# Strassen's seven products over half of K in three gates in place of one; the gated sum h in DRAM between the gates, the score tiles in a slot

## The chip, the core and the metric
The kernel runs on one core of a Trainium2 chip: TensorE (matmul), VectorE, ScalarE, GpSimd, and SyncE, whose queue issues most DMAs. The metric is the device time of one execution in microseconds, the median of several runs.

## What is computed
One layer of a hybrid decoder for 512 prompt rows and 8 x 4 = 32 sample rows, together 544 rows, with D = 2048 and branch width 512, in float32. Cut to what matters here:

```python
z = x @ w_in                       # 12 projections of 512 columns, 4 forget columns, 4 gates of 2048 columns
h = 0
for i, (o, g) in enumerate(branches):         # gMLP, convolution, FoX attention, memory attention
    gate = sigmoid(gate_pre[:, i*2048:(i+1)*2048])       # a (544 x 2048) @ (2048 x 2048) product each
    h = h + gate * ((o * silu(g)) @ w_branch[i])         # (544 x 512) @ (512 x 2048)
y = layer_norm(ALPHA * x + h @ w_out)
```
FoX attention of the sample rows reads 1024 past keys and values for each of 8 sequences from pages in DRAM.

## The kernel before
All matmuls take a weight tile of 128 x 128 as stationary operand and x transposed as moving operand, in two halves of 272 columns. Each float32 operand is split into a high and a low part, and a product is three matmuls (high-high, high-low, low-high).

**Pieces.** The work is a list of `Piece`s. A plain piece (`std_load`, `std_conv`, `std_mm`) is 256 rows of K by 256 output columns: 2 K tiles x 2 column tiles x 3 products x 2 halves = 24 matmuls, all at line 269. Its weights are loaded into `raw` (5 buffers) up to four pieces ahead of their split; ScalarE (L238) and VectorE (L239) split them into `whl` (4 buffers), three pieces ahead of their matmuls. A projection is 16 pieces. A gate (`add_gates`) is 8 blocks of 256 columns; a block is 8 pieces of the gate product (K = 2048) and 2 pieces of the branch product (K = 512). The accumulators are four PSUM banks, two for each column tile: the gate product leaves them through a sigmoid on ScalarE (L1034) into a tile `gs`, the branch product through a multiplication on VectorE (L1045 or L1047), and from the second gate on GpSimd adds the result to h (L1048). h lies in four slots of SBUF until the end.

**Strassen.** In six blocks of the last gate (`add_strassen`) the first half of K is done as a 2 x 2 block product in seven products in place of eight: pieces P1 to P4 in the order of `kinds`, 12 matmuls each (L387), then 4 plain pieces for the other half of K and 2 for the branch. Weight differences are made on VectorE (L358) from four `sw` tiles, the operands from x by `t_sx` (L335, 28 steps) in the first two blocks of that gate, into four slots.

**The order of the list**: Q_C, 4 forget columns, K_C, V_C, Q_M (16 pieces each), 32 pieces for the memory's keys and values, V_A, U_A, G_A (16 each), gate 0 (80), G_M (16), gate 3 (80), A_B, B_B, G_C (16 each), gate 2 (80), G_B (16), 4 pieces of the pointwise convolution, gate 1, the output projection. I name the gates by their number in the code: 0, 3, 2 and last 1.

**What runs between.** The order is written out by hand (`tc.manual_schedule`): all engines take their instructions in the order of the program. Ahead of a piece's matmuls two chains of side tasks (generators in `Side`) get steps: in a plain piece up to 2 of chain 0 and 1 of chain 1; a step that yields 1 ends its chain's turn for the piece. A third list, `side.vec`, is `v_scores`: 24 empty steps and then 1280 scores of the sample rows against their pages (one VectorE instruction each, L713), given out by `side.vector(rate)`: 4 per piece before gate 0, 5 after it, none in Strassen pieces, and one of two pieces in the memory's 32. It begins in the third piece of K_C. When the last score is issued, `t_decode("qc")` is added to chain 0: 5 steps for the bias (`t_bias`), 2 transposes, softmax, and from step 13 on 16 groups of V products (L865), each of two steps of one per piece. For every group GpSimd gathers four pages of V by indirect DMA (L884) into a slot, two groups ahead; the slots (18 of 8.7 KB per partition, for all large tiles) are given out in the order in which they come free. The first evacuation of G_C (`ev_gate`, L1004), at the end of its eighth piece, calls `side.finish` for the two attention tasks: what they have left is issued there at once. `t_b`, the convolution task (chain 1, from the end of B_B), makes 124 convolution steps (L1216, L1219), two to a step of the task, in G_C and gate 2, with no steps in pieces that follow the end of a product; behind them its tail (two means with jn, L1231 to L1236, square root, sigmoid). `t_a` is the gMLP's task in V_A to G_A.

## Time and profile before
| | us |
|---|---|
| median of 3 runs | 1955.72 |
| lowest, highest | 1955.38, 1957.82 |
| the profiled execution, its own time | 1958.77 |
| its span, first to last instruction | 1957.1 |
| TensorE busy | 1926.9 |
| VectorE busy | 1278.6 |

The profile is of one execution. Its page gives the busy time of each engine, the chain of work that ended last, and the costliest groups of instructions; the trace behind it answers for single stretches, lines and tiles. "Idle before" an instruction names what ended the wait. The engine names of the rows are PE (TensorE), PEld (its weight loads), DVE (VectorE), ACT (ScalarE), POOL (GpSimd) and SP (SyncE).

### The profile page before, as it was taken

The numbers are of one execution on the slowest core, as the hardware profiler recorded it, in microseconds if no ns is written. First come the engines' busy times: TensorE is split into PE (matmuls) and PEld (weight loads), VectorE is DVE, ScalarE is ACT, GpSimd is POOL, SyncE is SP. The second block draws the span as 40 slices with busy tenths as digits, with TensorE's granted clock in tenths as the row PEclk, the third lists the DMA queues.
The fourth block names the chain that finished last, engine by engine and source line by source line (L and its number), as shares of the span: only waits on it lengthen the run. The fifth ranks groups of instructions, "written<-read, shape, count | busy, mean of one in ns | idle before, by whom it ended". The sixth has DMA issues, their size and how long they took to land.

```text
span 1957.1 us, 38249 instructions
## 1 busy us (share of the span) xinstructions
PE 1926.9 (98%) x14615; PEld 1854.2 (95%) x14615; DVE 1278.6 (65%) x4201; ACT 642.2 (33%) x1208; POOL 233.3 (12%) x265
## 2 busy tenths in 40 slices
PE   8999999999999999999999999999999999999997
PEld 7999989999999899999999889999999999999985
DVE  3265787777776777877763238667645655466687
ACT  3222353344223222222222222222243333344442
POOL 0000000010000000121215430101110011010000
PEclk9999999999999999999999999999999999999999
DMA  5444465324555544444436663333323332346664
GB/s 162 107 119 119 137 199 148 104 77 128 166 168 171 183 136 116 138 131 123 138 105 193 191 194 86 88 87 88 91 76 87 103 96 67 108 130 216 201 216 159
DMA packets 217745, 261.84 MB, mean 134 GB/s; under 512 B 18251, under 2 KB 177499, under 8 KB 216761
## 3 DMA queue, kind: packets, MB, share of 16 engines
q1 hardware_dynamic: 206441, 224.55, 39.5%
q0 software_dynamic: 10544, 33.80, 5.6%
q8 instruction: 114, 1.87, 0.4%
q10 hardware_dynamic: 576, 1.05, 0.1%
q14 instruction: 70, 0.57, 0.1%
HBM read 250.85 MB, written 8.49 MB: 133 GB/s over the span
## 4 chain that ended last, share of the span: by engine, by line
PE 79%; DVE 4%; DMA 3%; issue 1%; ACT 1%; SPq 0%; POOL 0%; DVEq 0%; ACTq 0%; POOLq 0%
PE acc L269 65%; PE acc L1393 4%; PE acc L387 3%; PE acc L926 2%; DVE whl L239 1%; PE ps L865 1%; DMA raw<-in_w_out_dram 1%; DMA raw<-in_w_branch_dram 1%; DMA qb<-qqm 0%; DVE junk L713 0%; DMA vr<-in_cache_mem_v_dram 0%; PE ps L958 0%; ACT whl L238 0%; PE ps L979 0%; PE ps L616 0%
## 5 line engine op out<-in xcount | busy, mean ns | idle before, releaser
L269 PE MATMUL acc<-xh,whl 128*128 128x272 f32 x6784 | 1172.7, 291 | 3.2 <-DVE sg L1010 2.5
L269 PEld LDWEIGHTS acc<-xh,whl 128*128 128x128 f32 x6784 | 969.8, 190 | 22.5 <-ACT whl L238 7.5
L238 ACT ACTIVATE whl<-raw 128x512 fp32r<-128x512 f32 x640 | 403.0, 632 | 1045.8 <-PE acc L269 864.8
L269 PE MATMUL acc<-xl,whl 128*128 128x272 f32 x3392 | 702.1, 289 | 0.0
L239 DVE TENSOR_TENSOR whl<-raw,whl 128x512 fp32r<-128x512 f32 x640 | 445.3, 699 | 359.9 <-ACT whl L238 352.8
L269 PEld LDWEIGHTS acc<-xl,whl 128*128 128x128 f32 x3392 | 535.6, 189 | 0.0
L713 DVE CUSTOM_DVE_ANT_0 junk<-kr,qb 128x128 f32<-128x128 f32 x1280 | 379.6, 297 | 48.5 <-DMA qb<-qqm 7.6
L269 PE MATMUL acc<-bh,whl 128*128 128x272 f32 x1024 | 177.5, 289 | 2.0 <-ACT gs L1034 1.3
L1048 POOL TENSOR_TENSOR h<-h,gs 128x272 f32<-128x272 f32 x96 | 79.3, 855 | 602.0 <-DVE gs L1047 601.9
L269 PEld LDWEIGHTS acc<-bh,whl 128*128 128x128 f32 x1024 | 146.7, 189 | 3.8 <-ACT gs L1024 1.8
L884 POOL DMA_INDIRECT kr<-in_cache_k_dram,idx x64 | 65.7, 1027 | 683.6 <-DVE L L713 497.9
L269 PE MATMUL acc<-hh,whl 128*128 128x288 f32 x512 | 107.2, 299 | 0.2 <-DVE whl L239 0.2
L269 PE MATMUL acc<-bl,whl 128*128 128x272 f32 x512 | 105.7, 288 | 0.0
L1219 DVE SCALAR_TENSOR_TENSOR yb<-hb,wdwc,yb 128x512 f32<-128x512 f32 x120 | 93.4, 779 | 2.1
L269 PEld LDWEIGHTS acc<-hh,whl 128*128 128x128 f32 x512 | 83.5, 188 | 0.8 <-DVE whl L239 0.4
L713 DVE DVE_READ_ACCUMULATOR2_ANT L<- 128x1 f32 x1024 | 83.9, 82 | 0.0
L269 PEld LDWEIGHTS acc<-bl,whl 128*128 128x128 f32 x512 | 80.6, 189 | 0.0
L269 PE MATMUL acc<-hl,whl 128*128 128x288 f32 x256 | 75.6, 295 | 0.0
L884 POOL DMA_INDIRECT vr<-in_cache_v_dram,idx x64 | 65.4, 1023 | 57.2 <-PE ps L865 40.5
L1393 PE MATMUL acc<-whl,hh 128*128 128x512 f32 x216 | 68.1, 396 | 0.8 <-ACT whl L238 0.5
L239 DVE TENSOR_TENSOR whl<-sw,whl 128x512 fp32r<-128x512 f32 x42 | 33.2, 791 | 40.4 <-ACT whl L238 26.3
L1393 PEld LDWEIGHTS acc<-whl,hh 128*128 128x128 f32 x216 | 40.4, 189 | 10.2 <-ACT whl L238 1.0
(350 smaller groups left out, 1425.1 us busy)
## 6 DMA issues: line engine op xcount, KB each, us to landing
raw<-in_w_in_dram SPq DMA_DIRECT2D x422, 256.0 KB, 2.8
raw<-in_w_out_dram SPq DMA_DIRECT2D x128, 256.0 KB, 3.6
raw<-in_w_branch_dram SPq DMA_DIRECT2D x64, 256.0 KB, 2.7
qb<-qqc SPq DMA_DIRECT2D x32, 256.0 KB, 4.1
qb<-qqm SPq DMA_DIRECT2D x32, 256.0 KB, 4.0
sw<-in_w_in_dram SPq DMA_DIRECT2D x24, 256.0 KB, 4.6
raw<-in_w_mem_k_dram SPq DMA_DIRECT2D x16, 256.0 KB, 2.7
raw<-in_w_mem_v_dram SPq DMA_DIRECT2D x16, 256.0 KB, 3.4
```

The lines of the kernel that those rows point to most:

```text
L238: S.activation(out=hi, in_=src, func=AF.Copy)
L239: side.later(lambda: V.tensor_tensor(out=lo, in0=src, in1=hi.bitcast(F32), op=ALU.subtract))
L269: T.matmul(out=p.st[c][i][:, 0:hi - lo], lhsT=p.w[:, wp, k, c * 128:(c + 1) * 128], rhs=mv[mp][:, p.k0 + k, lo:hi], start=(p.first or (c, ...
L387: T.matmul(out=acc, lhsT=p.w[:, wp, i, :], rhs=mv, start=p.kind in ("P1", "P2", "P5") and i == 0 and wp == 0 and mp == 0, stop=i == n - 1 ...
L713: V.tensor_tensor_reduce(out=junk, in0=kr[:, n % 2, h * 128:(h + 1) * 128], in1=qb[:, t, h * 128:(h + 1) * 128], op0=ALU.mult, op1=ALU.add ...
L865: T.matmul(out=ob[32 * j:32 * j + 32, :], lhsT=PT[:, pg, 4 * g + j, :], rhs=vr[:, j, :], start=pg == 0, stop=pg == npg - 1 and not fox)
L884: G.indirect_dma_start(out=dst, out_offset=None, in_=src, in_offset=bass.IndirectOffsetOnAxis(ap=idx[:, j:j + 1], axis=0))
L926: T.matmul(out=mem["a", p.wi, j], lhsT=m[:, mp, (2 * (p.kt % 2) + j) * 128:(2 * (p.kt % 2) + j + 1) * 128], rhs=p.w[:, wp], start=p.kt == ...
L1048: G.tensor_tensor(out=hd, in0=hd, in1=s, op=ALU.add)
L1219: V.scalar_tensor_tensor(out=yv, in0=hv, scalar=wdw[:, j, c:c + 1], in1=yv, op0=ALU.mult, op1=ALU.add)
L1393: T.matmul(out=oacc[p.nb, j], lhsT=hhl[p.kt // 4][mp][:, p.kt % 4, o:o + 128], rhs=p.w[:, wp], start=p.kt == 0 and mp == 0 and wp == 0, st ...
```

## The change
- Strassen over the first half of K in all 8 blocks of gate 3, in blocks 1 to 6 of gate 2 and in blocks 1 to 7 of gate 1 (`STR`): 21 blocks in place of 6. The operands are made once, by `t_sx` in gate 0 from its 56th piece on, and stay in four slots.
- h is no longer kept in SBUF: each block's 128 x 1088 part is stored to DRAM (`hscr`) some pieces after the block's end and loaded at the start of the same block of the next gate, into a ring of two; in gate 1 it is loaded into its final place. The loads (`pre`) and stores (`behind`) are issued on SyncE's queue.
- The tiles of the scores and of the pages of K move from two `kt` buffers (of three) to one slot.
- The scores come at 5 per plain piece, in gate 3 at 4 per plain piece, and at one per Strassen piece.
- Strassen pieces P5, P6 and P2 give no step to chain 1. In the stretch of the convolution the plain pieces give chain 1 two steps, and `t_b` makes one convolution step per step; its tail waits until G_B.

```diff
@@ -84,6 +84,7 @@
         self.after = None
         self.evac = None
         self.fresh = None
+        self.pre = None
         self.__dict__.update(kw)
 
 
@@ -276,6 +277,8 @@
         n = p.steps
         if marks["dw"] <= p.i < marks["pw"] and pieces[p.i - 1].last:
             n = (n[0], 0)
+        elif marks["dw"] <= p.i < marks["pw"]:
+            n = (n[0], 2)
         side.step(n)
         side.vector(rate(p.i))
         for c in range(2):
@@ -368,6 +371,7 @@
 
     def s_mm(p):
         side.step(p.steps)
+        side.vector(1)
         s = p.s
         if p.kind == "P1":
             a, b_, c_, d = [accb() for _ in range(4)]
@@ -402,6 +406,8 @@
         order = ("P1", "P5", "P3", "P6", "P7", "P2", "P4")
         new = [Piece(src=src, kgs=kgs, kind=k, s=s, st=st_, load=s_load, conv=s_conv, mm=s_mm, steps=(1, 1), last=False,
                      whole=len(kgs) == len(movs)) for k in order]
+        for p in new[1::2]:
+            p.steps = (1, 0)
         for p, k in zip(new, kinds):
             p.mm = lambda _, q=[n for n in new if n.kind == k][0]: s_mm(q)
         rest = [g for g in range(2 * len(movs)) if g // 2 not in kgs]
@@ -412,7 +418,7 @@
             if p.last:
                 p.evac = lambda p=p: std_evac(p)
             new.append(p)
-        for p, f in zip(new[6:], after):
+        for p, f in zip(new[6:], after or ()):
             p.after = f
         pieces.extend(new)
         return s
@@ -678,8 +684,9 @@
     def v_scores():
         batches = [("qc", b, NPG) for b in range(3)] + [("qm", b, 2) for b in range(8)] + \
                   [("qc", b, NPG) for b in range(3, 8)]
-        S_["qc"] = kt_t([128, 1056], n="L")
-        kr = kt_t([128, 2, 512], n="kr")
+        lk = slot([128, 2176], n="lk")
+        S_["qc"] = lk[:, 0:1056]
+        kr = lk[:, 1056:2080].rearrange("p (j c) -> p j c", j=2)
         qb = slot([128, 4, 512], n="qb")
         pages = [(k, b, pg, i) for i, (k, b, n) in enumerate(batches) for pg in range(n)]
         done = {"qc": 0, "qm": 0}
@@ -1015,7 +1022,10 @@
             return rest
         return fn
 
+
     hacc = [None] * 4
+    hscr = [dram.tile([128, 2, 2, HALF], F32, name=f"h{m}") for m in range(8)]
+    behind = []
 
     def ev_str(c, hf, a, gs):
         if (c, hf) != (0, 1):
@@ -1023,8 +1033,24 @@
             a = gs
         S.activation(out=gs, in_=a, func=AF.Sigmoid)
 
-    def add_gates(i, br, first, afters=None, strassen=()):
-        sgof = {}
+    def add_gates(i, br, place, afters=None, strassen=()):
+
+        sgof, hof, ring = {}, {}, {}
+
+        def h_load(m):
+            if place == 1:
+                if m == 0:
+                    ring[0] = slot([128, 2, 2, 2, HALF], n="hr")
+                hof[m] = ring[0][:, m % 2]
+            else:
+                if m % 2 == 0:
+                    hacc[m // 2] = slot([128, 4, 2, HALF], n="h")
+                hof[m] = hacc[m // 2][:, 2 * (m % 2):2 * (m % 2) + 2]
+            SP.dma_start(out=hof[m], in_=hscr[m])
+
+        def h_store(m):
+            behind.append((3, lambda: SP.dma_start(out=hscr[m], in_=hof[m])))
+
         for m in range(8):
             sgof[m] = {}
 
@@ -1035,24 +1061,24 @@
 
             def ev_prod(c, hf, a, m=m):
                 gs = sgof[m]["gs"]
-
-                mt = 2 * m + c
-                if hacc[mt // 4] is None:
-                    hacc[mt // 4] = slot([128, 4, 2, HALF], n="h")
-                hd = hacc[mt // 4][:, mt % 4, hf, :]
                 s = gs[:, c, hf, :]
-                if first:
-                    V.tensor_tensor(out=hd, in0=a, in1=s, op=ALU.mult)
+                V.tensor_tensor(out=s, in0=a, in1=s, op=ALU.mult)
+                if place:
+                    hd = hof[m][:, c, hf, :]
+                    G.tensor_tensor(out=hd, in0=hd, in1=s, op=ALU.add)
                 else:
-                    V.tensor_tensor(out=s, in0=a, in1=s, op=ALU.mult)
-                    G.tensor_tensor(out=hd, in0=hd, in1=s, op=ALU.add)
+                    hof[m] = gs
 
             col = GATE + i * D + m * 256
+            k = len(pieces)
             if m in strassen:
                 sgof[m] = add_strassen(w_in[:, col:col + 256], xmov, ev_str, (0, 1), afters if m == 7 else ())
             else:
                 add_pair(w_in[:, col:col + 256], xmov, ev_sig, after=afters if m == 7 else None)
-            add_pair(w_branch[i, :, m * 256:(m + 1) * 256], [lambda: flat(B[br])], ev_prod)
+            if place:
+                pieces[k].pre = lambda m=m: h_load(m)
+            add_pair(w_branch[i, :, m * 256:(m + 1) * 256], [lambda: flat(B[br])], ev_prod,
+                     (lambda m=m: h_store(m)) if place < 2 else None)
 
 
     def ev_va(c, hf, a):
@@ -1218,9 +1244,10 @@
                 else:
                     V.scalar_tensor_tensor(out=yv, in0=hv, scalar=wdw[:, j, c:c + 1], in1=yv, op0=ALU.mult,
                                            op1=ALU.add)
-                if j % 2:
-                    yield
+                yield
         del B["hb"], B["hs"]
+        while "gb_on" not in B:
+            yield 1
         jn = s2([128, 128], n="jn")
         V.memset(jn, 1.0 / 128)
 
@@ -1454,26 +1481,28 @@
                 p.evac = lambda p=p: m_evac(p)
             pieces.append(p)
     marks = {}
+    STR = {3: range(8), 2: range(1, 7), 1: range(1, 8)}
     add_proj(V_A, ev_va, lambda: tasks.__setitem__("a", side.add(t_a(), 0)))
     add_proj(U_A, ev_ua, lambda: B.__setitem__("ua_done", 1))
     add_proj(G_A, ev_gate("ua", "brA", ("a",)))
     marks["gates"] = len(pieces)
-    add_gates(0, "brA", True)
+    add_gates(0, "brA", 0)
     add_proj(G_M, ev_gate("qm", "brM", ("am", "dqm")))
-    add_gates(3, "brM", False)
+    marks["gm"] = len(pieces)
+    add_gates(3, "brM", 1, strassen=STR[3])
     marks["conv"] = len(pieces)
     add_proj(A_B, ev_ab)
     add_proj(B_B, ev_bb, lambda: tasks.__setitem__("b", side.add(t_b(), 1)))
     marks["dw"] = len(pieces) + 8
     add_proj(G_C, ev_gate("qc", "brC", ("ac", "dqc")))
-    add_gates(2, "brC", False)
+    add_gates(2, "brC", 1, strassen=STR[2])
+    marks["gb"] = len(pieces)
     add_proj(G_B, ev_gb)
     marks["pw"] = len(pieces)
     for m in range(2):
         add_pair(I["w_pw"][0][:, m * 256:(m + 1) * 256], [lambda: flat(B["yhl"])],
                  lambda c, hf, a, m=m: ev_pw(2 * m + c, hf, a))
-    marks["last"] = len(pieces)
-    add_gates(1, "brB", False, [h_split(0), h_split(1), h_split(2)], range(2, 8))
+    add_gates(1, "brB", 2, [h_split(0), h_split(1), h_split(2)], STR[1])
     marks["out"] = len(pieces)
     for m in range(8):
         add_pair(w_out[:, m * 256:(m + 1) * 256], hmov, ev_out, done_out(m), parts=((0, 288),), steps=(1, 1))
@@ -1485,13 +1514,14 @@
             pieces.append(p)
 
     def rate(i):
-        return 4 if i < marks["gates"] else 5
+        return 4 if marks["gm"] <= i < marks["conv"] and STR[3] else 5
 
     at = {
         marks["conv"]: lambda: side.add(t_cconv(), 1),
         marks["pw"]: lambda: side.finish(tasks["b"]),
-        marks["last"]: lambda: tasks.__setitem__("sx", [side.add(t_sx((g,)), 1 - g) for g in (0, 1)]),
-        marks["last"] + 20: lambda: side.finish(*tasks["sx"]),
+        marks["gates"] + 55: lambda: tasks.__setitem__("sx", side.add(t_sx((0, 1)), 0)),
+        marks["gm"]: lambda: side.finish(tasks["sx"]),
+        marks["gb"]: lambda: B.__setitem__("gb_on", 1),
         marks["out"] + 1: h_split(3),
         marks["out"] + 3: fin_x(0, 0),
         marks["out"] + 4: fin_x(0, 1),
@@ -1565,7 +1595,15 @@
                 at[i]()
             while nconv <= min(i + 3, n - 1):
                 conv()
+            if p.pre:
+                p.pre()
             p.mm(p)
+            for _ in range(len(behind)):
+                n_, f = behind.pop(0)
+                if n_:
+                    behind.append((n_ - 1, f))
+                else:
+                    f()
             if p.after:
                 p.after()
         pieces[-1].evac()
```

## Rows read from the trace of the kernel before

**Rows 1.** The page's first part: busy time, its share of the span, instructions.
```profile
PE 1926.9 (98%) x14615; PEld 1854.2 (95%) x14615; DVE 1278.6 (65%) x4201; ACT 642.2 (33%) x1208; POOL 233.3 (12%) x265
```

**Rows 2.** The chain of waits, asked for the stretch from 1206 to 1420 us (gate 2): start, duration, what.
```profile
1205.93 212.23 PE acc L269 x1694
```

**Rows 3.** The chain of waits in gate 1, from 1480 to 1760 us: start, duration, what; L269 is a plain piece's matmul, L387 a Strassen product's.
```profile
1539.26 30.56 PE acc L269 x240
...
1598.83 10.54 PE acc L387 x84
...
1619.83 0.69 DVE sw L358
1620.52 0.36 DVE gs L1022
...
1620.90 0.72 ACT gs L1024 x2
...
1627.84 10.54 PE acc L387 x84
```

**Rows 4.** Busy time by stretch: from, to, length, then busy time (and instructions) of TensorE, its weight loads, VectorE, ScalarE, GpSimd, the granted clock, the share of the DMA engines and GB/s. The stretches are a plain block of gate 3, one of gate 2 and a Strassen block of gate 1.
```profile
860.00:890.00 30.00, 30.00 (x241) 30.00 (x241) 23.25 (x115) 7.59 (x14) 6.48 (x8) 1.00 0.47 135
1265.00:1295.00 30.00, 30.00 (x242) 30.00 (x241) 20.61 (x31) 7.53 (x15) 3.44 (x4) 1.00 0.33 88
1599.00:1628.00 29.00, 28.86 (x230) 28.64 (x229) 15.34 (x26) 10.48 (x21) 3.41 (x5) 1.00 0.32 92
```

**Rows 5.** VectorE in order of time, in gate 3 (with scores, L713), gate 2 (convolution steps, L1219, first without and then with GpSimd's additions beside them) and a plain piece of gate 1: start, duration, what, and in brackets the idle time before and what ended it.
```profile
891.40 0.69 DVE L239 TENSOR_TENSOR whl<-raw,whl 128x512 fp32r<-128x512 f32 x1 [0.77 <-ACT whl L238]
892.01 0.28 DVE L713 CUSTOM_DVE_ANT_0 junk<-kr,qb 128x128 f32<-128x128 f32 x1
...
892.34 0.29 DVE L713 CUSTOM_DVE_ANT_0 junk<-kr,qb 128x128 f32<-128x128 f32 x1
...
1401.43 1.53 DVE L1219 SCALAR_TENSOR_TENSOR yb<-hb,wdwc,yb 128x512 f32<-128x512 f32 x2
...
1412.85 1.07 DVE L239 TENSOR_TENSOR whl<-raw,whl 128x512 fp32r<-128x512 f32 x1
1413.84 2.04 DVE L1219 SCALAR_TENSOR_TENSOR yb<-hb,wdwc,yb 128x512 f32<-128x512 f32 x2
...
1587.08 0.69 DVE L239 TENSOR_TENSOR whl<-raw,whl 128x512 fp32r<-128x512 f32 x1 [2.31 <-ACT whl L238]
```

**Rows 6.** Groups of instructions by line, shapes kept apart: count, busy time in us, mean ns of one, idle time before.
```profile
L239 DVE TENSOR_TENSOR whl<-sw,whl 128x512 fp32r<-128x512 f32 x42 | 33.2, 791 | 40.4 <-ACT whl L238 26.3 <-DMA raw<-in_w_branch_dram 13.8
...
L358 DVE TENSOR_TENSOR sw<-sw,sw 128x512 f32<-128x512 f32 x24 | 16.6, 691 | 0.6
...
L1047 DVE TENSOR_TENSOR gs<-acc,gs 128x272 f32<-128x272 f32 x96 | 37.6, 435 | 13.4 <-PE acc L269 12.3
...
L1048 POOL TENSOR_TENSOR h<-h,gs 128x272 f32<-128x272 f32 x96 | 79.3, 855 | 602.0 <-DVE gs L1047 601.9
```

**Rows 7.** Three source lines, the scores, A_B's evacuation and the decode's V products: count, duration in ns (least/median/most), first and last start in us, shapes.
```profile
L713 DVE CUSTOM_DVE_ANT_0 junk<-kr,qb x1280: 254/291/1276, 110.6 to 1013.3; 128x128 f32<-128x128 f32 x183
...
L1148 ACT ACTIVATE ab<-acc x8: 392/396/398, 1052.4 to 1083.1; 128x272 f32<-128x272 f32 x8
...
L865 PE MATMUL ps<-vr,PTs x160: 590/593/618, 641.1 to 1169.0; 128*32 128x512 f32 x160
```

**Rows 8.** TensorE in order of time: the gMLP task's wait, the end of the decode task in the middle of G_C, and a wait in gate 2.
```profile
383.78 0.29 PE L1114 MATMUL ps<-cA,vta 128*32 128x16 f32 x2 [3.02 <-DVE cA L1110]
...
1168.48 1.06 PE L865 MATMUL ps<-vr,PTs 128*32 128x512 f32 x8
...
1175.56 0.74 PE L269 MATMUL acc<-xh,whl 128*128 128x272 f32 x2 [1.39 <-DVE sg L1010]
...
1441.24 0.68 PE L269 MATMUL acc<-bh,whl 128*128 128x272 f32 x2 [1.28 <-ACT gs L1034]
```

**Rows 9.** GpSimd in order of time: gathers of a page of V for the decode task.
```profile
1124.29 0.94 POOL L884 DMA_INDIRECT vr<-in_cache_v_dram,idx  x1 [2.16 <-PE ps L865]
...
1144.21 0.95 POOL L884 DMA_INDIRECT vr<-in_cache_v_dram,idx  x1 [0.30 <-issue]
1145.46 0.95 POOL L884 DMA_INDIRECT vr<-in_cache_v_dram,idx  x1 [0.30 <-issue]
```

**Rows 10.** DMA issues: count, KB each, median us from issue to landing.
```profile
raw<-in_w_in_dram SPq DMA_DIRECT2D x422, 256.0 KB, 2.8
...
vr<-in_cache_mem_v_dram SPq DMA_DIRECT2D x4, 1024.0 KB, 5.5
...
vr<-in_cache_v_dram,idx POOLq DMA_INDIRECT x64, 4.2
```

**Rows 11.** Busy time by stretch around the wait at 380.8 us (columns as in rows 4; the third number from the end is the granted clock, 1.00 being 2.4 GHz).
```profile
370.00:400.00 30.00, 26.51 (x184) 25.57 (x183) 25.26 (x92) 11.84 (x24) 2.94 (x3) 0.89 0.28 78
380.00:383.00 3.00, 0.76 (x7) 0.54 (x5) 2.90 (x10) 0.63 (x1) 0.00 (x0) 1.00 0.13 18
383.00:392.00 9.00, 8.22 (x41) 8.05 (x42) 5.83 (x27) 1.91 (x2) 0.00 (x0) 0.62 0.31 83
```

**Rows 12.** Busy time by stretch, of the instructions that write or read the tile in which Strassen's operands are made, in gate 1: from, to, length, VectorE's busy time (and instructions), ScalarE's, the granted clock, the DMA share and GB/s.
```profile
1505.00:1555.00 50.00, 20.12 (x28) 4.77 (x8) 1.00 0.40 108
```

**Rows 13.** The source line of the ScalarE copy within a mean of the convolution task (columns as in rows 7).
```profile
L1233 ACT ACTIVATE jt<-ps x4: 397/398/398, 1418.8 to 1445.3; 128x272 f32<-128x272 f32 x4
```

## The prediction
> **What bounds the kernel now.** I read the page's first part first: TensorE is busy for 1926.9 of 1957.1 us (98%), VectorE for 65% [rows 1]. Since a pipelined TensorE looks busy even when it is slow, I then asked whether it runs at its own pace. The chain through gate 2 says yes: 1694 matmuls of one kind stand in a row in 212.23 us with no other work between them, so 0.1253 us each [rows 2]. A plain block of a gate (10 pieces of 24 matmuls, 240 in all) is therefore 30.07 us. So in the gates the time is the number of matmuls, as long as nobody else is late; what has to be asked is where the change makes somebody late.
>
> **What the seven products save.** A Strassen block issues 84 matmuls in place of 96 for half of K: 228 per block. At the pace above that is 28.57 us, but gate 1 already runs such blocks, and the chain shows what they take: the 84 products begin at 1598.83 and again at 1627.84, 29.01 us apart [rows 3]. The missing 0.44 us is seen in the same rows: the branch product's first matmuls wait for the sigmoids that empty the banks, and these for VectorE, which has a split and a difference of operands to do first. The gain is 30.07 - 29.01 = 1.06 us per block, not 1.50. The change has 21 such blocks for 6, so 15 x 1.06 = **-15.9 us** if the new ones run as undisturbed as the old.
>
> **Do they?** VectorE is busy for 15.34 us of an undisturbed Strassen block, 23.25 us of a plain block of gate 3 and 20.61 of one of gate 2 [rows 4]. Gate 3 carries attention scores: back to back they start 0.33 us apart [rows 5], and 7 x 1 + 6 x 4 = 31 of them come per block: 15.34 + 10.4 = 25.7 of 29.0 us. In gate 2 the depthwise convolution gives 14 steps of 0.77 us [rows 5]: 15.34 + 10.8 = 26.1. Both fit on average. But the seven products last 10.54 us and their VectorE work is 7 splits x 0.79, 4 differences x 0.69, one addition of 0.43, the last two gate products 0.87 [rows 6], and 7 scores, 2.34: 11.9 us. VectorE falls 1.4 us behind in each product phase and has to have run ahead before. On top comes GpSimd's addition to h: beside it a split took 1.07 us for 0.69, and two convolution steps 2.04 for 1.53 [rows 5], 0.9 us in all; the additions fall just into the product phase of the next block. Nothing here reaches below nothing, since no work leaves those phases. The ends are 0 and 2.3 us per block (14 blocks: 0 to 32); I take 0.3, near the lower end, since VectorE stands idle for 2.31 us before the split of a plain piece in gate 1 [rows 5], and scores, which wait for no TensorE result, can move there: **+4 us**.
>
> The Trainium skill (SBUF — State Buffer, section "Who interferes with whom") says that a VectorE instruction with two SBUF inputs and a GpSimd instruction that reads SBUF exclude each other for the whole instruction. By that rule four additions of 0.86 us could hold VectorE for 3.4 us per block where the row shows 0.9; 14 blocks times 2.5 us is an estimate of 35 us more, and it would turn the sum into the third rival below. The slowed rows agree with the rule in kind, not in size.
>
> **What is moved: the sample's attention.** This decides my sum. The scores (1280, after 24 empty steps) are rationed by pieces, and when the last is issued the decode task starts, which needs 45 steps at one per piece; its V products are steps 13, 15, ... 43. It must be finished when the first column of G_C is evacuated, in piece 39 after gate 3's end, where whatever is left is issued in one go.
> Before: (46 + 16 + 48) pieces x 4 = 440 rations by the start of gate 0, 400 in gate 0, 80 in G_M, so the 1305th (24 + 1280, and one that ends the list) comes in piece 76 of gate 3, four pieces before its end. The rows agree: the last score starts at 1013.3, A_B's first evacuation (8 pieces after gate 3) is at 1052.4 [rows 7]. Step 43 then falls into piece 39: its product is at 1168.48, and the wait at the gate is 1.39 us [rows 8]. It fits exactly, with no spare piece.
> After: 110 x 5 = 550, 400 and 80 by the start of gate 3, then 8 x 31 = 248: 1278. The last 27 take six pieces of A_B. The decode starts **nine pieces later**; by piece 38 it has done step 33, eleven of sixteen V groups. Five groups remain for the gate. What the rows say about one: four gathers of 1.25 us each from start to start on GpSimd, about 4.2 us from issue to landing, and each group's gathers wait for the product that frees a buffer [rows 9, 10] (18 slots: 8 for x, 4 for Strassen's operands where h had 4, q, hb, the decode's weights, yb: two are left for V). A group is 1 us on TensorE [rows 8]. In the burst the first two are there: 2 us. The third's gathers start after the first product and have landed 1 + 3.75 + 4.2 = 9 us from the start; the fourth's follow on GpSimd, 5 us later, and the fifth's another 5: its product ends at 20, and the copy and transposes behind it, no longer under other work, add 1. Of these 21 us 5 are products that exist today: 16 us idle. If yb takes its slot only when written, the third group's gathers run before the burst: 11. I take 13.5. TensorE's clock pays as well: after the 3.02 us of idle time at 380.8 the granted clock fell to the lower of its two levels (1.2 of 2.4 GHz) and was 0.62 on average over the next 9 us [rows 8, 11], which cost 0.38 x 9 = 3.4 us. Together **+17 us** (14 to 20).
>
> The Trainium skill (TensorE: Matmul & The Clock Gate, section "HAM oscillation — how this bites in real kernels") says that each wait in a row of waits finds the array slow again. By that rule the two products between the three waits, 2 us, run at half speed as well: an estimate of 19 instead of 17. The one drop in the trace agrees; no row shows a series.
>
> **The smaller parts.** The score ration rises from 4 to 5 in the pieces ahead of gate 0. Around the gMLP task's wait at 380.8 VectorE is already busy 25.26 of 30 us, and 2.90 of 3 within it [rows 11]; one more score per piece over some six to ten pieces is 2 to 3 us there, if TensorE waits for all of it; 0 to 4, I take **+2**.
> Strassen's operands are made in gate 0 beside five scores per piece: in gate 1 their 28 VectorE instructions took 20.12 us [rows 12], over 28 steps 0.72 us per piece; with 1.67 for scores, 0.61 for the split [rows 5] and 0.17 for the gate product this is 3.2 us in a piece of 3.0. Between 0 and 28 x 0.2 plus the waits of each block's evacuation, 8: **+3**. In gate 1 the same work is gone, where the block behind its end took 30.56 us [rows 3], 0.5 over its pace: **-0.5**.
> The convolution task's tail moves into G_B at two steps per piece. A mean is two steps, with a ScalarE copy of 0.40 us between two TensorE products [rows 13]; in one piece TensorE has nothing in between. Four of these at 0.4 to 1.0: **+2**. A wait of 1.28 us for ScalarE at 1441.24, in the tail's old place [rows 8], goes: **-1.3**.
> h through DRAM is 24 stores and 24 loads of 128 x 4352 B, 0.56 MB. A load is issued at the block's start on the queue of the weight loads and needed a block later; a store is issued four pieces on, when GpSimd's four additions (4 x 0.86 us [rows 6]) are done. Behind each on that queue stand the weights for pieces four and more ahead, 6 us even of products. A transfer of 1 MB landed in 5.5 us and one of 0.25 MB in 2.8 [rows 10], so I place these near 4: hidden, 0; 0 to 4 if the cover is short. Moving the scores' tiles frees two buffers which no wait in the chain asks for: 0.
>
> **Sum**: -15.9 + 4 + 17 + 2 + 3 - 0.5 + 2 - 1.3 = +10.3 us. On the profiled execution (span 1957.1, 1958.8 with what lies around it) that gives 1969.1; the median shown, 1955.72, is 3.05 lower, so I predict a median of **1966 us**.
>
> **Rivals.**
> 1. *The burst is hidden.* If two or three more slots are free in the burst, GpSimd gathers ahead (it waits for buffers only, as it did twice at 1144.21 [rows 9]), and no long idle time comes. Then 17 falls to about 1: 1950, faster. It decides from the point at which GpSimd has the thirteenth group before the gate. Against it is the count of slots. Chance 0.19.
> 2. *All cover holds* and only the undisturbed saving and the two waits gone remain: 1955.7 - 15.9 - 1.8 = 1938, 0.06.
> 3. *VectorE becomes the bound* in the product phases of gates 3 and 2: 14 x 2.3 = 32 in place of 4: 1994. For it, 11.9 + 0.9 us of work in 10.54; against it, the means of 25.7 and 26.1 in 29.0. 0.12.
> 4. *Half of the burst*, with the small parts near nothing: 1955, no change. 0.08.
> My forecast keeps 0.55, with its own range 1957 to 1978.
>
> **How the numbers follow.** Range 1945 to 1982: from rival 1 with its small parts at their lower ends to the forecast with the burst at 20 and VectorE's lag at twice my value; rivals 2 and most of 3 are left out (about 0.17). A measurement of this kernel can tell about 0.2%, 4 us, from no change. Faster: rival 1 but 0.03 of it, and rival 2: 0.22. Slower: forecast but 0.05, and rival 3: 0.62. The same: 0.16.
>
> **What would show it.** Right: TensorE idle for 11 us or more in the middle of G_C, waiting for V gathers, with granted clock near 0.5 behind it; the last score after gate 3's last block; 1764 products; product phases 29.1 to 29.6 us apart in gates 3 and 2. Wrong: V products evenly spaced up to G_C's first evacuation; blocks above 30 us in gates 3 or 2 (rival 3); the queue of loads waiting for GpSimd.

## The result and the profile after

The changed kernel takes **1968.82 us** (median of 4 runs, 1967.71 to 1970.1), the kernel before 1955.66 beside it: a ratio of 1.0065, interval 1.0048 to 1.0083. It is slower, by 13 us; the prediction said 1966 (+10.3). The profiled execution has a span of 1968.1 us against 1957.1, so 11.0 us are there to be found.

The page's first part after [rows 1]:

```profile
PE 1922.8 (98%) x14435; PEld 1838.2 (93%) x14435; DVE 1362.6 (69%) x4366; ACT 683.7 (35%) x1296; POOL 237.4 (12%) x265
```

TensorE has 180 instructions less, as 15 blocks of 12 fewer products should give, and is busy for 4.1 us less, while the span grew by 11. So one looks for waits. I cut both traces at the same events (the first evacuation of each projection) and took the length of each stage after minus before:

| stage | change, us |
|---|---|
| start to V_A's evacuation, and on to U_A's | +4.1, +0.4 |
| G_A to G_M (gate 0) | +3.3 |
| G_M to A_B (gate 3) | -5.3 |
| A_B to B_B, B_B to G_C | -3.0, -0.5 |
| G_C to G_B (gate 2) | +15.6 |
| G_B to the pointwise product, on to the first output (gate 1), to the end | -0.2, -2.9, -0.5 |

**The blocks do what was expected.** Busy time by stretch (columns as in [rows 4]), one Strassen block of gate 3 and two of gate 2, from the first product of one block to that of the next:

```profile
858.16:887.17 29.01, 28.87 (x230) 28.65 (x229) 23.72 (x88) 10.47 (x20) 5.32 (x7) 1.00 0.47 148
...
1250.03:1279.12 29.09, 28.95 (x231) 28.69 (x229) 24.88 (x40) 10.47 (x20) 3.87 (x5) 1.00 0.41 129
1279.12:1308.19 29.07, 28.93 (x230) 28.71 (x229) 25.21 (x40) 10.46 (x20) 3.81 (x4) 1.00 0.41 130
```

A block takes 29.00 to 29.13 us from start to start in place of 30.07 [rows 2], with VectorE busy for 23.7 to 25.2; the last block of either gate, with plain pieces behind it, took 28.59 and 28.73. That makes 13 of the 14 new blocks in these gates. The exception is gate 3's first, 34.4 us. TensorE there:

```profile
794.78 0.39 PE L391 MATMUL acc<-xh,whl 128*128 128x272 f32 x1 [1.93 <-DVE sg L1017]
...
801.31 0.39 PE L391 MATMUL acc<-sh,whl 128*128 128x272 f32 x1 [1.73 <-ACT gs L398]
```

It waits first for VectorE's reading of G_M's banks, then for ScalarE. Behind each of the two waits the granted clock fell to the lower of its two levels (0.50 from 795.7 to 799.0 and from 802.5 to 805.9 us, 1.00 between them), as it did in [rows 11]; over the stretch it is 0.69 on average:

```profile
792.00:795.00 3.00, 1.07 (x8) 0.86 (x7) 2.86 (x13) 0.69 (x2) 0.00 (x0) 1.00 0.00 0
795.00:806.00 11.00, 9.27 (x47) 8.86 (x47) 8.18 (x26) 4.83 (x11) 1.17 (x1) 0.69 0.43 129
806.00:812.00 6.00, 6.00 (x50) 6.00 (x49) 4.00 (x17) 2.53 (x4) 0.00 (x0) 1.00 0.72 220
```

What ScalarE had ahead of that copy (L398) is in its timeline: G_M's split, four times in turn with VectorE (multiplication L1020, copy L235, difference L236), and only then the weights' conversion for the next products (L239) and the copy:

```profile
796.15 0.43 ACT L235 ACTIVATE bh<-sg 128x272 fp32r<-128x272 f32 x1 [2.70 <-DVE sg L1020]
797.44 0.43 ACT L235 ACTIVATE bh<-sg 128x272 fp32r<-128x272 f32 x1 [0.86 <-DVE sg L1020]
798.73 0.43 ACT L235 ACTIVATE bh<-sg 128x272 fp32r<-128x272 f32 x1 [0.86 <-DVE sg L1020]
800.02 0.43 ACT L235 ACTIVATE bh<-sg 128x272 fp32r<-128x272 f32 x1 [0.86 <-DVE sg L1020]
800.36 0.61 ACT L239 ACTIVATE whl<-sw 128x512 fp32r<-128x512 f32 x1
800.87 0.38 ACT L398 ACTIVATE gs<-acc 128x272 f32<-128x272 f32 x1
```

**The decode's burst is there.** The scores (one source line, columns as in [rows 7]) end 33 us later than before, after gate 3's last block:

```profile
L720 DVE CUSTOM_DVE_ANT_0 junk<-lk,qb x1280: 252/291/1279, 104.3 to 1046.8; 128x128 f32<-128x128 f32 x183
```

and TensorE in the middle of G_C, in order of time ([rows 8] has the same place before, where one wait of 1.39 us stood):

```profile
1172.62 5.91 PE L872 MATMUL ps<-vr,PTs 128*32 128x512 f32 x26
1178.75 1.05 PE L872 MATMUL ps<-vr,PTs 128*32 128x512 f32 x2 [0.22 <-DMA vr<-in_cache_v_dram,idx]
1180.15 1.05 PE L872 MATMUL ps<-vr,PTs 128*32 128x512 f32 x2 [0.35 <-DMA vr<-in_cache_v_dram,idx]
1181.48 3.36 PE L872 MATMUL ps<-vr,PTs 128*32 128x512 f32 x6 [0.28 <-DMA vr<-in_cache_v_dram,idx]
1185.30 1.04 PE L872 MATMUL ps<-vr,PTs 128*32 128x512 f32 x2 [0.46 <-DMA vr<-in_cache_v_dram,idx]
1186.68 1.05 PE L872 MATMUL ps<-vr,PTs 128*32 128x512 f32 x2 [0.34 <-DMA vr<-in_cache_v_dram,idx]
1187.66 1.06 PE L876 MATMUL ps<-rows,PnT 32*32 32x512 f32 x8
1189.62 0.63 PE L862 MATMUL ps<-ident,Oall 128*128 128x128 f32 x4 [0.91 <-DVE Oall L882]
1190.92 0.74 PE L270 MATMUL acc<-xh,whl 128*128 128x272 f32 x2 [0.67 <-DVE sg L1017]
```

18.3 us without a product of G_C. One should not add up the brackets: they hold 3.2 us, because the products of one page after the other start as each lands, and a line such as the first counts as busy although its last products start 0.4 to 0.7 us apart. The length of the stretch, and what stood elsewhere before, is the price.

### The profile page after: what moved, and what is told of

Read it like the earlier page. It is cut to its first block, busy times and chain, and to the rows that moved or that the text cites. A ratio compares the mean times of both kernels' runs of the same rounds, so it can differ in the third digit from the quotient of the medians.

```text
span 1968.1 us, 38309 instructions
## 1 busy us (share of the span) xinstructions
PE 1922.8 (98%) x14435; PEld 1838.2 (93%) x14435; DVE 1362.6 (69%) x4366; ACT 683.7 (35%) x1296; POOL 237.4 (12%) x265
## 4 chain that ended last, share of the span: by engine, by line
PE 64%; DVE 9%; DMA 3%; ACT 2%; issue 2%; POOL 1%; SPq 0%; DVEq 0%; ACTq 0%; POOLq 0%
PE acc L270 47%; PE acc L391 11%; PE acc L1420 3%; DVE whl L240 2%; DVE junk L720 2%; DMA raw<-in_w_in_dram 1%; ACT whl L239 1%; PE ps L872 1%; DVE sw L361 1%; DMA qb<-qqm 1%; ACT gs L1034 1%; POOL vr L891 1%; DMA raw<-in_w_out_dram 1%; DMA vr<-in_cache_mem_v_dram 0%; DVE bl L236 0%
## 5 line engine op out<-in xcount | busy, mean ns | idle before, releaser
L239 ACT ACTIVATE whl<-raw 128x512 fp32r<-128x512 f32 x580 | 364.8, 631 | 848.0 <-PE acc L270 630.3
L270 PE MATMUL acc<-xl,whl 128*128 128x272 f32 x2912 | 602.8, 288 | 0.0
L270 PEld LDWEIGHTS acc<-xl,whl 128*128 128x128 f32 x2912 | 459.5, 189 | 0.0
L720 DVE CUSTOM_DVE_ANT_0 junk<-lk,qb 128x128 f32<-128x128 f32 x1280 | 381.4, 298 | 44.6 <-DMA qb<-qqm 6.5
L240 DVE TENSOR_TENSOR whl<-sw,whl 128x512 fp32r<-128x512 f32 x147 | 115.1, 789 | 73.0 <-ACT whl L239 71.2
L891 POOL DMA_INDIRECT lk<-in_cache_k_dram,idx x64 | 63.9, 999 | 685.1 <-DVE lk L720 564.0
L239 ACT ACTIVATE whl<-sw 128x512 fp32r<-128x512 f32 x147 | 92.4, 628 | 150.8 <-PE acc L270 78.8
L391 PE MATMUL acc<-sh,whl 128*128 128x272 f32 x672 | 133.2, 293 | 1.7 <-ACT gs L398 1.7
L391 PEld LDWEIGHTS acc<-sh,whl 128*128 128x128 f32 x672 | 108.8, 192 | 2.4 <-ACT gs L398 2.0
L391 PE MATMUL acc<-sl,whl 128*128 128x272 f32 x336 | 97.9, 291 | 0.0
L720 DVE DVE_READ_ACCUMULATOR2_ANT lk<- 128x1 f32 x1024 | 83.8, 82 | 0.0
```

What stands on the lines that cost most here:

```text
L239: S.activation(out=hi, in_=src, func=AF.Copy)
L240: side.later(lambda: V.tensor_tensor(out=lo, in0=src, in1=hi.bitcast(F32), op=ALU.subtract))
L270: T.matmul(out=p.st[c][i][:, 0:hi - lo], lhsT=p.w[:, wp, k, c * 128:(c + 1) * 128], rhs=mv[mp][:, p.k0 + k, lo:hi], start=(p.first or (c, ...
L391: T.matmul(out=acc, lhsT=p.w[:, wp, i, :], rhs=mv, start=p.kind in ("P1", "P2", "P5") and i == 0 and wp == 0 and mp == 0, stop=i == n - 1 ...
L720: V.tensor_tensor_reduce(out=junk, in0=kr[:, n % 2, h * 128:(h + 1) * 128], in1=qb[:, t, h * 128:(h + 1) * 128], op0=ALU.mult, op1=ALU.add ...
L891: G.indirect_dma_start(out=dst, out_offset=None, in_=src, in_offset=bass.IndirectOffsetOnAxis(ap=idx[:, j:j + 1], axis=0))
```

## The experiments

They ran at four times on chips on which the kernel before took 1956.4 to 1962.4 us; so I compare ratios to it, and give microseconds as the ratio's difference times 1956: against 1 for a version of the kernel before, against 1.0065 for a version of the changed kernel. A ratio's interval is some 3 us to either side, so two versions 3 us apart are not told apart by it alone; there the stages have to speak too. Stages are of one profile each and are good to 1 or 2 us: ten kernels, the changed one among them, have the same code up to V_A's evacuation, and reached it at 329.0 to 332.8 us.

**The burst alone, in the kernel before.** It starts the decode nine pieces later and does nothing else.
```diff
-        for _ in range(24):
+        for _ in range(69):
```


> The kernel before, with 45 more empty steps ahead of the scores, so that at 5 per piece the decode task starts nine pieces later, as in the changed kernel, and nothing else is different. Theory (the late start alone costs the burst): 1955.7 + 14 = 1969 to 1971 us, with five V groups together in G_C. Rival (the burst is as long as it is because the changed kernel has fewer free slots for V, so that GpSimd can't gather ahead; the kernel before, with its scores' tiles outside the slots and no ring for h, has two more): four groups have landed before the gate, and the time is 1958 to 1961.


Measured: 1964.03 us, ratio 1.0035 (1.0022 to 1.0047), +7 us. TensorE at the gate:
```profile
1164.06 3.60 PE L865 MATMUL ps<-vr,PTs 128*32 128x512 f32 x22
1168.51 1.69 PE L865 MATMUL ps<-vr,PTs 128*32 128x512 f32 x4 [0.84 <-DMA vr<-in_cache_v_dram,idx]
...
1182.26 0.75 PE L269 MATMUL acc<-xh,whl 128*128 128x272 f32 x2 [0.67 <-DVE sg L1010]
```
The stretch is 18.2 us, as long as in the changed kernel, so the rival (fewer buffers) falls. But the theory's price falls too. By stages: G_C to G_B +16.4, and gate 3 -3.5, A_B -3.0, B_B -0.6, from which the V products and the decode's other steps have gone: net **+9.3**. The start is 2.3 us shorter in this profile, which brings the 9.3 down to the 7 of the medians; whether the 45 empty steps make it so was not tested.

**More scores in gate 3**, in the changed kernel.
```diff
     def rate(i):
-        return 4 if marks["gm"] <= i < marks["conv"] and STR[3] else 5
+        return 5
```


> The changed kernel, with 5 scores instead of 4 per plain piece of gate 3 (37 per block in place of 31), so that the last score is issued some ten pieces before A_B and the decode task has its 45 pieces before the gate of G_C. Theory (the decode starts too late, and its V products stand in a burst at that gate, about 13.6 us): 1968.8 - 13.6 = 1955 us, 1952 to 1959, with V products evenly spaced and no wait for V in G_C. Rival 1 (VectorE has no room: 15.34 + 37 x 0.33 = 27.7 of 29.0 us per block, and runs behind in the product phases): the burst goes, but the blocks of gate 3 grow by up to 2.0 us each, 1962 to 1971. Rival 2 (the waits in G_C come from the gathers' own pace, not from the decode's start): 1969, no change.


Measured: 1965.67, ratio 1.0045 (1.003 to 1.006), -4 us. No wait for V is left in G_C: its stage is 16.9 us shorter, and with A_B (+3.4), B_B (+0.9) and the decode's part in gate 3 (7.5 longer, less the 4.4 below) that is a net of 9.5, the same as the other experiment gave. But rival 1 is right beside it: the blocks of gate 3 took 0.56 us more each (the first 0.5). A block:
```profile
887.87:917.43 29.56, 29.11 (x228) 28.67 (x228) 25.46 (x100) 10.46 (x21) 5.58 (x6) 1.00 0.48 138
```
VectorE is busy for 25.5 of 29.6 us, and the block is late all the same. Its timeline shows where: it idles in the x pieces, and has no gap in the branch pieces ahead of the products, where splits and differences queue behind five scores and the bank is read last:
```profile
907.54 0.08 DVE L720 DVE_READ_ACCUMULATOR2_ANT lk<- 128x1 f32 x1
908.39 0.69 DVE L240 TENSOR_TENSOR whl<-sw,whl 128x512 fp32r<-128x512 f32 x1 [0.77 <-ACT whl L239]
...
915.61 0.69 DVE L240 TENSOR_TENSOR whl<-sw,whl 128x512 fp32r<-128x512 f32 x1
916.33 0.69 DVE L361 TENSOR_TENSOR sw<-sw,sw 128x512 f32<-128x512 f32 x1
916.94 0.78 DVE L1065 TENSOR_TENSOR gs<-acc,gs 128x272 f32<-128x272 f32 x2
```

**Four blocks of gate 3 plain again.**
```diff
-    STR = {3: range(8), 2: range(1, 7), 1: range(1, 8)}
+    STR = {3: range(4), 2: range(1, 7), 1: range(1, 8)}
```


> The changed kernel, with the seven products in the first four blocks of gate 3 only; its last four blocks are plain, with 40 scores each in place of 31. The last score then comes some two pieces before the end of gate 3, about where it was in the kernel before. Theory (burst by late decode): 4 x 1.06 us of saving are lost and 13.6 us of burst come back: 1968.8 + 4.2 - 13.6 = 1959.5 us, 1957 to 1963, less time with more products. Rival (the loss lies in the Strassen blocks themselves or in the path of h): 1968.8 + 4.2 = 1973.


Measured: 1965.21, ratio 1.0045 (1.0031 to 1.006), -4 us: 48 products more and less time. The sign speaks for the theory; with a net burst of 9.3 in place of 13.6 the expectation would have been 1964.

**Six scores at the start of gate 0**, so that the decode is in time and gate 3 is left alone.
```diff
+        if marks["gates"] <= i < marks["gates"] + 50:
+            return 6
```


> The changed kernel, with 6 scores instead of 5 per piece in the first 50 pieces of gate 0, before Strassen's operands are made there; gate 3 keeps 4 per plain piece. The last score then comes some five pieces before the end of gate 3, as in the kernel before. Theory (the burst by itself costs 9.3 us, what the kernel before lost by nine pieces of delay, and gate 0's plain blocks, where VectorE is busy for 23 of 30 us, have room for ten more scores of 0.33 us): 1968.8 - 9.5 = 1959 us, 1957 to 1961, with gate 3's blocks at 29.0 us and no wait for V in G_C. Rival 1 (VectorE's order, not its mean, decides, as in gate 3 at 5 per piece, where a block took 29.57 in place of 29.01): gate 0 grows by up to 0.6 us per block, 1962. Rival 2 (the burst is worth the 13.6 us of the stage's account): 1955.


Measured: 1967.39, ratio 1.0054 (1.0041 to 1.0068), hardly a gain. The burst is gone (G_C to G_B 16.9 shorter, gate 3's later blocks at 29.00), but gate 0 is 5.3 us longer. A single wait carries it, at its first block's end, where 0.90 us had stood:
```profile
526.02 0.94 PE L270 MATMUL acc<-xh,whl 128*128 128x272 f32 x2 [4.19 <-DVE gs L1065]
```

**Fewer scores in G_M**, more in the x pieces of gate 3's later blocks, on top of that.
```diff
+        if marks["gm"] - 16 <= i < marks["gm"]:
+            return 4 if i < marks["gm"] - 8 else 3
+        if marks["gm"] <= i < marks["conv"]:
+            k = i - marks["gm"]
+            return 5 if k >= 13 and k % 13 < 11 else 4
```


> The kernel with 6 scores per piece at the start of gate 0, and in addition 4 and then 3 scores per piece in place of 5 in G_M, ahead of the first Strassen block; the 24 scores are made up by 5 in the first four plain pieces of the later blocks of gate 3 (35 per block). Theory (the first block's 34.4 us in place of 29.0 come from VectorE being behind since G_M, with the clock's drop after the two waits): 5 us less than with 6 scores at the start of gate 0 alone, 1954 us, 1952 to 1957, the first block at 29 to 30.5 us, and the other blocks still at 29.0, since the products' phase and the two pieces ahead of it get no score more. Rival 1 (the wait at the first block comes from G_M's own evacuation and Strassen's first differences, whatever the scores): no change against that kernel, 1959. Rival 2 (35 scores slow the blocks as 37 did, by 0.4 us): 1957.


Measured: 1964.89, ratio 1.0041 (1.0027 to 1.0055). Two answers. The first block still took 34.7 us: the wait for VectorE is gone, and the one for ScalarE's copy behind G_M's split is 3.66 us (1.73 in the changed kernel, 3.26 in the last experiment). So G_M's scores are not what makes the block long; that leaves the chain of the last evacuation, which the next experiment tests. And 35 scores per block, none more in the branch pieces, cost nothing:
```profile
860.47:889.48 29.01, 28.87 (x230) 28.65 (x229) 24.89 (x96) 10.49 (x20) 5.66 (x7) 1.00 0.48 148
```

**Gate 3's first block plain.**
```diff
+    STR = {3: range(1, 8), 2: range(1, 7), 1: range(1, 8)}
```


> The changed kernel, with the first block of gate 3 plain (the seven products in its other seven blocks); the scores stay at 4 per plain piece, 40 in this block. Theory (G_M's last evacuation is a chain of four times 1.29 us between ScalarE and VectorE, ahead of the next blocks' splits on both queues; three converted plain pieces, 9 us, cover its 5.2 us and three converted products, 4.5 us, don't; with the clock's drop behind it, 5.4 us): 1.06 us of saving are lost and 5.4 come back, and two pieces of the decode's delay with 1 to 2 us of burst: 1968.8 - 4.3 - 1.5 = 1963 us, 1961 to 1965. Rival (the first block is late because of what Strassen's first differences need, wherever they start, so that the wait moves to the second block): 1969 to 1970.


Measured: 1970.19 where the kernel before took 1961.0, ratio 1.0048 (1.0029 to 1.0067), -3 us. Gate 3's stage is 3.6 us shorter with 12 products more. The wait for ScalarE's copy is gone; one of 1.44 us for VectorE stands at the second block, so a part of the rival may hold. Of the expected 6 us half was seen. The interval is wide, and the profiled run has a loss of its own: from 1150 to 1157 us TensorE's matmuls have gaps of up to 1.58 us that the profile puts down to issue, and the stage from B_B to G_C is 6.5 us longer than in the changed kernel.

**The tail's means**, first with one break per mean:
```diff
             S.activation(out=t, in_=b[:, 0:HALF], func=AF.Copy)
-            yield
+            yield 1
```


> The changed kernel, in which the two products of a mean of the convolution task's tail are put into different pieces (the first step of a mean ends the chain's steps of that piece), so that ScalarE's copy between them has a piece's other products beside it. Theory (four waits of 0.91 to 0.97 us for that copy in G_B): 1968.8 - 3.5 = 1965.3 us. Rival (the tail then ends some pieces later, what is left is issued at once ahead of the pointwise product, and the wait moves there): 1968 to 1970.


Measured: 1978.38, ratio 1.0105 (1.0088 to 1.0122): slower by 8 us. The break moved the other steps: now the mean of the squares stood in one piece with the subtraction and the square it needs, and TensorE waited twice, 2.58 and 2.68 us, for ScalarE's square, and then 2.49 us for VectorE at the end of G_B. Then with all steps apart:
```diff
-            yield
+            yield 1
```
(in all three places of the means and variances)


> The changed kernel, with every step of the two means and variances in the convolution task's tail in a piece of its own (eight pieces of G_B; before, one break per mean moved the wait from the copy to the square). Theory (four waits of 0.91 to 0.97 us for ScalarE's copies in G_B): 1968.8 - 3.5 = 1965.3 us. Rival (the last steps are then issued at once ahead of the pointwise product, or its operand is late): 1968 to 1972.


Measured: 1965.93, ratio 1.0049 (1.0035 to 1.0062), -3 us as expected by the medians; the four waits are gone. The tail's stages (G_C to the pointwise product) show less of it, 1.2 us, and 2.7 in the experiment on the early ration and the tail, where the same edit stands.

**h twice.**
```diff
-            behind.append((3, lambda: SP.dma_start(out=hscr[m], in_=hof[m])))
+            behind.append((3, lambda: [SP.dma_start(out=d[m], in_=hof[m]) for d in (hscr, hscr2)]))
```
(and each load issued twice)


> The changed kernel, in which every store of h goes to two places in DRAM and every load of h is made twice into the same tile: 48 transfers of 0.56 MB more on the queue of the weight loads. Theory (h's way through DRAM is hidden, 0 us in the sum): 1968.8 us, 1967 to 1970.5. Rival (the queue has no spare time for a transfer of this size, and weights come late): 0.5 us or more for each, 1980 or more.


Measured: 1970.5, ratio 1.0073 (1.0059 to 1.0087); the spans are 1968.2 and 1968.1 us. 48 further transfers cost nothing that can be told.

**Both causes undone**: first block plain, scores in time.
```diff
+        k = i - marks["gm"]
+        if 10 <= k and i < marks["conv"]:
+            return 5 if (k - 10) % 13 < 11 else 4
+        return 5
```


> The same kernel with a plain first block in gate 3, with 5 scores per piece in that block and in the first four plain pieces of each Strassen block (50 and 35 in place of 40 and 31), which left the blocks at 29.01 us; the last score then comes some seven pieces before the end of gate 3. Theory (the burst's net price is 9 us): 1963 - 8 = 1955 us, 1953 to 1958, the sum of both causes undone, no wait for V in G_C. Rival (what the burst cost comes back as other waits in A_B and B_B, where the V products and their copies then stand beside the evacuations): 1959 or more.


Measured: 1962.9 where the kernel before took 1961.0, ratio **1.001** (1.0001 to 1.0019), 7.4 us less than with the first block alone. No wait for V is left in G_C; the last group of V products takes about 1 us:
```profile
1174.94 1.07 PE L872 MATMUL ps<-vr,PTs 128*32 128x512 f32 x8
1175.94 1.06 PE L876 MATMUL ps<-rows,PnT 32*32 32x512 f32 x8
```
Five scores in the plain block, however, left VectorE late by 4.5 us at the first product phase behind it, where the wait had been 1.44.

**The early ration and the tail besides.**
```diff
+        if i < marks["gates"] and (pieces[i].mm is m_mm or marks["ua"] <= i < marks["ga"]):
+            return 4
+        if marks["gates"] <= i < marks["gates"] + 50:
+            return 4 if i < marks["gates"] + 10 else 6
```


> The same kernel as with the decode in time, and besides: 4 scores per piece in the memory projections' pieces and in U_A, as in the kernel before; 4 in the first block of gate 0 and 6 in its next four; and the steps of the means in the convolution task's tail in pieces of their own. Theory (the early score ration costs 4 us in the wait for the memory prompt and for the gMLP task, the tail 3 us): 1955 - 4 - 3 = 1948 us, 1945 to 1952, below the kernel before. Rival (the early waits come from the order of the queues and not from the fifth score, and gate 0 has no room for six): 1953 or more.


Measured: 1959.19 where the kernel before took 1961.0, ratio **0.9994** (0.9984 to 1.0004), equal to the kernel before. The start is 5.2 us shorter than in the changed kernel up to V_A (and 0.6 on to U_A), the tail's stages 2.7 shorter than in the last experiment. The wait at the first product phase of gate 3 is still there (4.38 us), and gate 0 is 4.5 longer than in the last experiment: its room for six scores isn't there in the later blocks either (waits of 1.58, 1.96 and 0.75 us for VectorE at three blocks' ends).

**A last combination.**
```diff
-            for _ in range(2):
+            for _ in range(1 if fox and i % 5 in (1, 3) else 2):
                 yield 1
...
+        if pieces[i].mm is m_mm:
+            return 4
+        k = i - marks["gm"]
+        if -8 <= k < 10:
+            return 4 if k < 6 else 3
+        if 10 <= k and i < marks["conv"]:
+            return {7: 5, 8: 6, 9: 5, 10: 5}.get((k - 10) % 13, 4)
+        return 5
```


> A version built from what the other runs showed, all in the same order of pieces: gate 3's first block plain; 5 scores per piece again in U_A and in all of gate 0 (six cost waits in gate 0's blocks), 4 in the memory projections' pieces and in G_M's last eight, 4 and then 3 in gate 3's first block, so that VectorE isn't behind at the first product phase; 36 scores in the Strassen blocks of gate 3, none of them more in the two branch pieces and the product phase; six of the sixteen V groups of the decode task take one piece instead of two, so that a decode that starts two pieces after gate 3's end needs 39 pieces; and the means' steps in pieces of their own. Theory (four separate causes that add up: gate 3's start 4.3, the burst 9, the memory prompt's wait 3, the tail 3): 1968.8 - 19 = 1950 us on a chip where the kernel before takes 1956, a ratio of 0.997. Rival 1 (36 scores are too many, as 37 were, or VectorE is late again at the first product phase): 1954 to 1957. Rival 2 (GpSimd's gathers, 5 us per group, don't keep up with the shorter V pieces, and a burst remains): 1955 to 1959.


Measured: 1973.25 where the kernel before took 1962.42, ratio 1.0054 (1.0041 to 1.0066). The theory is refuted, and neither rival names why. The first product phase was in time. But in the first Strassen block VectorE now waited for a load of queries; the block's evacuation stands behind the scores in its queue, came late, and the block took 34.7 us again:
```profile
836.86 0.29 DVE L720 CUSTOM_DVE_ANT_0 junk<-lk,qb 128x128 f32<-128x128 f32 x1 [5.70 <-DMA qb<-qqc]
```
The larger part, 14 us, lies from 1085 to 1175 us, in A_B, B_B and the start of G_C, where the V groups now come faster. One wait there has a name (2.19 us for ScalarE's evacuation of A_B). Besides it TensorE has gaps that the profile puts down to issue, 5.5 us in all; the granted clock is 1.00 while the largest of them stand, and 0.57 over the 4 us behind:
```profile
1160.53 0.29 PE L270 MATMUL acc<-xl,whl 128*128 128x272 f32 x1
1161.71 0.29 PE L270 MATMUL acc<-xl,whl 128*128 128x272 f32 x1 [0.89 <-issue]
```
What holds them stays open. They are of the kind seen with the first block plain; but the kernel with both causes undone has gathers at a DMA share of up to 0.90 in the same place and no such gaps.

## Why the prediction was right, step by step

**The mechanism was right, several sizes were not, and they cancelled.** That the sum came near the result is in part luck: the burst was priced 7.6 us too high, and VectorE's lag, the early scores, the tail and a step that the prediction lacks make up for it. Each term as predicted, and as the runs show it:

| term | predicted | measured | from |
|---|---|---|---|
| 15 more Strassen blocks | -15.9 | -15.3 | eight blocks of 29.01 (gate 3), six of 29.1 (gate 2), one more of 29.01 (gate 1) |
| VectorE late in the product phases | +4 | 0 in 13 blocks, +7.3 at one | blocks after: 5.4 in gate 3's first, 1.9 waited ahead of it |
| decode's burst at G_C | +17 | +9.4 net | stages of the kernel before with a late decode (9.3; 7 by the medians) and of five scores in gate 3 (9.5) |
| early scores at 5 | +2 | +4.5 | stages; the mean of ten kernels is +4.0; two with 4 are 5.3 shorter than that mean |
| Strassen's operands in gate 0 | +3 | +3.3 | stage of gate 0 |
| gate 1 without them | -0.5 | -1.8 | its stage, less the block's 1.06; 1.2 of it also in the kernel before with a late decode, whose code there is the same |
| tail of the convolution | +2 - 1.3 | +2.9 | four products 0.8 late, one 1.15 at G_B's end, less the old 1.4 (start to start) |
| convolution's first steps in G_C | none | +1.5 | below |
| h through DRAM | 0 | 0 | h twice |
| sum | +10.3 | +11.8, where 11.0 are to be found | |

**The largest error is the burst's price.** Place, length (18.5 us taken, between 16 and 21; 18.3 seen) and cause were as written: five groups, the third's gathers already under way. What I subtracted for work that exists today was 5 us, one per product group. The runs show 7.1 us leaving gate 3, A_B and B_B in the kernel with only the decode delayed (3.5 + 3.0 + 0.6): not only V products are moved, but the decode's other steps with them. The clock's share was too large as well. I priced it by the wait at the gMLP task, 3.4 us. By stretch (columns as in [rows 4]) the clock stood at its upper level through the burst and fell behind it:
```profile
1172.00:1178.00 6.00, 5.87 (x32) 1.54 (x30) 0.00 (x0) 0.69 (x2) 3.97 (x5) 1.00 0.77 249
1178.00:1185.00 7.00, 5.76 (x12) 0.69 (x10) 0.00 (x0) 0.00 (x0) 4.54 (x5) 1.00 0.73 199
1185.00:1191.00 6.00, 3.79 (x17) 0.93 (x17) 1.40 (x4) 0.00 (x0) 0.00 (x0) 1.00 0.10 34
1191.00:1194.00 3.00, 3.00 (x14) 2.84 (x15) 2.05 (x6) 0.80 (x2) 0.00 (x0) 0.60 0.01 3
1194.00:1197.00 3.00, 3.00 (x22) 3.00 (x21) 1.92 (x5) 1.28 (x4) 0.00 (x0) 0.83 0.00 0
```
3 x 0.40 + 3 x 0.17 = 1.7 us. The Trainium skill (TensorE: Matmul & The Clock Gate, section "HAM oscillation — how this bites in real kernels") says of a kernel whose waits last several microseconds that the array is slow again behind each of them. That does not describe this row: the waits in its brackets are 0.2 to 0.9 us, and the array didn't slow between them. It does fit the start of gate 3, where each of two waits of 1.9 and 1.7 us has a stretch at 0.50 behind it.

**VectorE's term was too small and wrong in kind.** I spread 4 us over 14 blocks; the product phases took the load, at 31 and at 35 scores, because scores run ahead in the x pieces, as the prediction said they could. It overlooked the seam ahead of the first block: the last evacuation of G_M is four links of 1.29 us between ScalarE and VectorE, ahead of the next weights' conversions on both queues. Three converted plain pieces (9 us) cover it, three converted products (4.5 us) don't. Gates 2 and 1 have a plain first block, and TensorE waits for ScalarE in neither (ahead of gate 2 it waits 1.61 us for VectorE, 1.08 before). That this seam is the cause is shown as far as the stage goes (3.6 us back with 12 products more); that the whole 7.3 are due to it is not, since a wait of 1.44 us stayed behind. The third rival's rate was refuted by the blocks. The rule of the Trainium skill (SBUF — State Buffer, section "Who interferes with whom") would by the prediction's estimate have made it 35 us, 2.5 us per block, of which no block of gate 3 or 2 but the first shows anything. VectorE is slowed beside GpSimd's additions here too, by about 1.5 us per block (in the block from 858.16 us a split took 1.25 us for 0.69, and two scores 0.70 and 0.86 for 0.29), and the block is 29.01 us all the same.

**The early term was too small and in the wrong place.** I priced the fifth score at the gMLP task's wait. It cost more at the memory prompt, whose transposes waited 1.95 us for a load, and behind which the clock was at 0.72 for 6 us:
```profile
289.69 0.52 PE L918 MATMUL ps<-ident,mr 128*128 128x128 f32 x3 [1.95 <-DMA mr<-in_mem_prompt_dram]
```
In all ten kernels with five scores TensorE waited 2.1 to 2.9 us for these loads, in the two with four 0.51 us and not at all. That load stands on SP behind the query loads, which wait for scores: so, as I read the order of the queue, a later score delays a transfer that has nothing to do with it; no run takes the two apart.

**One step was missing.** At two steps per piece the convolution's first steps (1.99 and 1.19 us on VectorE, with a split 3.9 us in a piece of 3.0) make VectorE late in G_C: a wait of 0.76 us at 1209 us that wasn't there, and one at the second evacuation 0.5 us longer.

Of the rivals, the first (the burst hidden, 1950) shows itself as a version, not as the result: in time, the kernel took 1.001 of the kernel before, not 0.997. The largest single part of the difference that shows is the wait of 4.5 us at the first product phase, where the scores that bring the decode in time take VectorE's room. Of the signs named, the place of the burst, the last score and the 1764 products came; the blocks of gate 3, 29.00 us apart, lie below the 29.1 to 29.6 that were to show the forecast right. No version here beats the kernel before by more than can be told; the best (0.9994) equals it.

## What to carry to other kernels

When a task is rationed by pieces of other work, making those pieces fewer delays the task: count its steps again to its deadline before counting what the shorter pieces save. A burst's price is its length less all work that leaves the stages before it, not less its last products only. And an engine's room is not its mean idle time: the same five scores were free in the pieces where VectorE waited for weights and cost 0.56 us per block in the two ahead of a phase of short pieces, so look at the seam, where a chain of the last stage meets pieces that convert half as far ahead.

## What the hardware showed that I had not expected

The granted clock stayed at 1.00 through 18 us in which TensorE waited again and again for 0.2 to 0.9 us, and fell only after the last wait (0.60 and 0.83 over the next 6 us). Two waits of 1.9 and 1.7 us at the start of gate 3 were each followed by a stretch at 0.50. And TensorE can run late without any wait that the profile names: in the last combination its matmuls had gaps of up to 0.89 us put down to issue, spread over some 70 us, while V pages were gathered, and with the first block plain gaps of up to 1.58 us within 7 us; it remains open by what.
